# Hybrid decoder layer: values and output features first for one token tile, the last tile's mean from the weights' row sums

## The chip, the cores and the metric

The kernel runs on one core of one Trainium2 chip. The metric is the device time of one execution in microseconds; several runs are given by their median. A profiled execution gives, beside its own time, the span from the first to the last instruction and what each engine did in it: PE (TensorE, matmuls, with its weight loads as PEld), DVE (VectorE), ACT (ScalarE), POOL (GpSimd) and SP, whose queue issues most DMAs.

## The reference

One layer of a hybrid decoder trunk, all in float32, with 512 prompt tokens and 8 sample tokens (one new token for each of 8 running sequences):

```python
h = jnp.einsum('bte,ed->btd', x, w_in)          # 1024 -> 3600 columns
qa, ka, va, za, ga, qb, kb, vb, gb = jnp.split(h, split_points, axis=-1)
o_a = gla_chunked(qa, ka, va, log_a, s0, chunk) # gated linear attention, 4 heads, then RMS norm
o_b = dilated_attention(...)                    # 8 heads of 64, three (window, dilation) patterns
mix = concat([o_a * silu(ga), o_b * silu(gb)])
y = jnp.einsum('bte,ed->btd', mix, w_out)       # 1024 -> 1024
x_new = layer_norm(ALPHA * x + y, ln_g, ln_b)   # over the 1024 features
```

Outputs are the new residual stream of prompt and sample tokens, the states of the linear attention, and the window keys and values. The change touches three places: the two value projections `va` and `vb` (512 columns each), the output projection, and the layer norm of the last 128 prompt tokens.

## The kernel before

**Precision.** Each float32 operand of a large matmul is split into a high part (rounded to the type fp32r) and a low part (the rest). A product is three matmuls, high by high, high by low and low by high, accumulated over the eight 128-row tiles k of the contraction (`three`, line 622). So a unit of output, one PSUM bank, is 24 matmuls. A matmul has a stationary operand of up to 128 columns, which a weight load brings into the array, and a moving operand that streams past it.

**Tokens.** The 520 tokens stand in the columns of `xh` and `xl` in the order: prompt tiles 0 and 1 (256 columns), the 8 sample tokens, prompt tiles 2 and 3. The first 264 columns are one half, `TS[0]`, with `TW[0]` = 264; the last 256 are the other.

**Feature first or token first.** Where the weights are stationary and the tokens stream, the result has features in its partitions; the sample tokens ride along as eight more columns. Where a tile of 128 tokens is stationary and the weights stream, the result has tokens in its partitions. Values and output are wanted token first, but the sample tokens are wanted feature first. `token` (line 640) therefore does the first half of the tokens feature first: for each of two feature blocks of 128 a unit of 24 matmuls with 264 moving columns. `turn` (line 659) copies the 256 prompt columns out of PSUM and turns them with two PE transposes for each block. Tiles 2 and 3 are then done token first, 24 matmuls with 256 moving columns each. There are four such groups: `vb0`, `vb1`, `va0`, `va1`. The evacuations are made by `vb_into` (line 1102), which also splits the values and stores them, and `va_into` (line 1085).

**Output projection.** Mix tiles, split like all operands, meet the weights `wo[0]` and `wo[1]`, 512 columns each. `out_first` (line 1512) does eight units feature first, 128 features and 264 tokens each; the first five take their k tiles 0 to 3 (attention) one after another, then their k tiles 4 to 7 (linear attention), so that the latter may come later. `out_turn` (line 1533) copies a unit, keeps the eight sample columns in `yts` and turns the rest by two transposes. `out_unit` (line 1500) does tiles 2 and 3 token first: (2, 0) and (2, 512) and (3, 0) with 512 moving columns, (3, 512) and (3, 768) with 256.

**Layer norm.** `out_evac` (line 1552) adds a piece from PSUM to ALPHA times the residual and takes statistics for every 256 columns. When a tile's four are there, `norm` (line 1599) merges them, takes the reciprocal root by Ln and Exp on ACT and one Newton step, centres, scales and stores. For the last tile the Newton step runs on ACT, and the final pass is cut in three, each with its own store.

**What sets the order.** The kernel's tasks are generators. A planner in Python (`Plan`, line 197) runs them at build time: it asks each task for its next instruction, estimates when that could start by a cost for each kind of instruction (`Op`, line 82) and fixed delays between engines (lines 76 to 80), and issues the one that could start first; ties go by the priorities `PRIO` (line 72), where a lower number comes first. All queues are therefore written in the order the planner chose. `At(name, n)` holds a task in planning until a mark was set n times; it is no wait on the chip, where only the data dependencies count. `dense` (line 695) is the one task that writes nearly all large matmuls in a fixed sequence: queries, keys, values `vb`, gates `gb`, values `va`, gates `ga`, output. `split` (line 416) and `Group` (line 459) load weights and split them, the high part on ACT, the low part on DVE. `keys_store`, `ln_rows` and `residual` (lines 1065, 1480, 1489) issue the key stores, the loads of the norm's rows, and the loads of the residual tiles.

Every instruction is issued at line 368, so a profile's rows are told apart by tile names: `ps_vb_f` and `ps_va_f` are the feature-first units of the values, `ps_vb` and `ps_va` the token-first ones, `ps_yf` and `ps_y` the same for the output, `ps_turn` and `ps_yt` their transposes.

Of the kernel before, what the change touches and what calls it, by code (L numbers as in the profile page):

```python
# [72 lines left out]
    wload=3, wsplit=4, decay=48.3, res_s=8, res=8, level=22, keys_out=2, logit=25.7, value=20, fills=9, bias_table=7.3, gla_levels=7.6, gla_diagonal=7.7, gla_state=24, gla_queries=25, strips=14, sample_queries=48, sample_softmax=8.7, sample_values=46, sample_gla=11, mix_sample_a=8.7, mix_sample_b=16, ln_rows=17, keys_store=17.5, gla_out=26, sample_v=9.2, mix_tiles=33.5, scores=31, softmax=34.2, weighted=30, mix_a=18, mix_b=19, norm3=11, norm=9)  # L73


FROM_POOL = 1000.0
TO_PE, FROM_PE, OTHER, AFTER_DMA, WITHIN = 600.0, 250.0, 150.0, 500.0, 120.0
LATE = 600.0
# [294 lines left out]
def trunk(ctx: ExitStack, tc: tile.TileContext, xT, xp, xs, state, ck, cv, w_in, wab, gnorm,  # L373
# [61 lines left out]
    eps, minus3 = cst("eps", [P, 1]), cst("minus3", [P, 1])  # L435
# [23 lines left out]
    class Group:  # L459
# [20 lines left out]
        def part(self, name):  # L480
            tags = ("w",)
            if self.src is w_out:

                tags += ("sv",) * (plan.marks["sample"] == 2) + ("pt",) * (plan.marks["ob1"] == HB) + ("g",)
            return (yield Need(tags, name + self.name, [P, self.kk, self.w], F32R, spare=tags[-1] == "g"))

        def split(self, i, raw):
            a = yield from self.part(f"hi{i}_")
            b = yield from self.part(f"lo{i}_")
            self.tiles.append((a, b))  # L490
            n = self.n
            for k in range(0, self.kk, n):
                yield from split(raw[:, k:k + n, :], a[:, k:k + n, :], b[:, k:k + n, :])
# [111 lines left out]
    def fills():  # L605
        yield V.memset(rb.bitcast(F32)[64:66], 1.0)
        yield V.memset(eps, LN_EPS)
        yield V.memset(minus3, -3.0)
# [31 lines left out]
    def token(g, evac_f, evac):  # L640

        for f in range(2):
            fs = slice(f * P, f * P + P)
            ps = yield bank("d", f"ps_{g.name}f{f}")
            for k in range(KT):
                yield g.at(k)
                h, l = xh[k][:, TS[0]], xl[k][:, TS[0]]
                yield from three(ps[:, :TW[0]], k, ((g.hi[k][:, fs], h), (g.hi[k][:, fs], l), (g.lo[k][:, fs], h)))
            add(evac_f(ps, f), 2)
        for t in (2, 3):  # L650
            ps = yield bank("d", f"ps_{g.name}{t}")
            ts = slice(NB + t * P, NB + t * P + P)
# [6 lines left out]
    def turn(ps):  # L659

        f = yield Need("t1", "feat", [P, GW])
        yield copy(f, ps[:, :GW])
        free(ps)
        o = yield bank("t", "ps_turn")
        for t in range(2):
            yield T.transpose(o[:, t * P:t * P + P], f[:, t * P:t * P + P], ident)
        return o, f
# [27 lines left out]
    def dense():  # L695
# [47 lines left out]
        units = [(g, f) for g in range(4) for f in range(2)]  # L743
# [321 lines left out]
    def keys_store():  # L1065

        yield At("kw", 8)
        yield At("y0_done", 1)
# [16 lines left out]
    def va_into(i):  # L1085
        def evac_f(ps, f):
            c = slice(i * GW + f * P, i * GW + f * P + P)
            yield copy(vat[:, 2 * i + f, :], ps[:, GW:TW[0]])
            mark("vat")
            ps, f_t = yield from turn(ps)  # L1090
            free(f_t)
            yield copy(B["va0"][:, :, c], ps[:, :GW].rearrange("p (t c) -> p t c", t=2))
            mark("va_done")
            free(ps)

        def evac(ps, t):
            yield copy(B["va1"][:, t - 2, i * GW:i * GW + GW], ps)
            free(ps)
            mark("va_done")
        return evac_f, evac  # L1100

    def vb_into(i):
        def parts_of(o, x):
# [3 lines left out]
        def evac_f(ps, f):  # L1107
            c = slice(i * GW + f * P, i * GW + f * P + P)
            yield copy(vnt[:, 2 * i + f, :], ps[:, GW:TW[0]])
            mark("vnt")  # L1110
            ps, raw = yield from turn(ps)
            yield from parts_of(B[f"vhl{i}0"][:, :, 2 * f:2 * f + 2], ps[:, :GW].rearrange("p (t h d) -> p t h d", t=2, d=64))
            mark(f"vb{i}0")
            yield copy(raw, ps[:, :GW])
            free(ps)
            yield D.dma_start(vw_p[:GW, c].rearrange("(t p) c -> p t c", p=P), raw.rearrange("p (t c) -> p t c", t=2))
            free(raw)

        def evac(ps, t):
            yield from parts_of(B[f"vhl{i}1"][:, t - 2], ps.rearrange("p (h d) -> p h d", d=64))  # L1120
            mark(f"vb{i}1")
# [5 lines left out]
        return evac_f, evac  # L1127
# [352 lines left out]
    def ln_rows():  # L1480
        yield At("y0_done", 1)
# [7 lines left out]
    def residual(t):  # L1489
# [7 lines left out]
        yield D.dma_start(y, xp[t * P:t * P + P, :])  # L1497
        mark(f"y{t}")

    def out_unit(t, c, w):  # L1500
        u, tl, cs = t // 2, slice((t % 2) * P, (t % 2) * P + P), slice(c % 512, c % 512 + w)
        g = wo[c // 512]
        ps = yield bank("d", f"ps_y{t}{c // GW}")
        for k in range(KT):
# [4 lines left out]
            yield from three(ps[:, :w], k, ((mh, hi), (mh, lo), (ml, hi)))  # L1509
        add(out_evac(t, c // GW, ps[:, :w]), 2)  # L1510

    def out_first(*units):
# [3 lines left out]
        for g, f in units:  # L1516
            ps.append((yield bank(("d", "s"), f"ps_yf{g}{f}")))
            yield from out_half(g, f, ps[-1], range(4))
        for (g, f), p in zip(units, ps):
            yield from out_half(g, f, p, range(4, KT))  # L1520
            add(out_turn(g, f, p), 2)

    def out_half(g, f, ps, ks):
        w, c = wo[g // 2], g % 2 * GW + f * P
        for k in ks:
# [3 lines left out]
            mh, ml = (B[f"m{x}{'ba'[k // 4]}0"][:, k % 4, :] for x in "hl")  # L1529
# [3 lines left out]
    def out_turn(g, f, ps):  # L1533
        feat = yield Need("t1", "feat_y", [P, GW])
        yield copy(feat, ps[:, :GW])
        yield copy(yts[:, 2 * g + f, :], ps[:, GW:TW[0]])
        mark("yts")
        free(ps)
        if f == 0:
            yield from make(f"yt{g}", bank("t", f"ps_yt{g}"))  # L1540
        else:
            yield At(f"yt{g}")
        for t in range(2):
            yield T.transpose(B[f"yt{g}"][:, t * GW + f * P:t * GW + f * P + P], feat[:, t * P:t * P + P], ident)
        free(feat)
        mark(f"yt_in{g}")
        if plan.marks[f"yt_in{g}"] == 2:
            plan.share(B[f"yt{g}"], 2)
            for t in range(2):
                add(out_evac(t, g, B[f"yt{g}"][:, t * GW:t * GW + GW]), 2)  # L1550

    def out_evac(t, g, ps):
# [8 lines left out]
        if plan.marks[f"y{t}_done"] == 4:  # L1561
            add(norm(t), PRIO["norm3"] if t == 3 else PRIO["norm"])
# [36 lines left out]
    def norm(t):  # L1599
# [4 lines left out]
        var, last = mv[:, 1:2], t == 3  # L1604
# [5 lines left out]

        def centre(c):
            yield V.scalar_tensor_tensor(y[:, c], y[:, c], mv[:, 0:1], B["gamma"][:, c], op0=ALU.subtract, op1=ALU.mult)

        def finish(c):
            return V.scalar_tensor_tensor(y[:, c], y[:, c], rstd, B["beta"][:, c], op0=ALU.mult, op1=ALU.add)

        yield At("ln", 3)
        if last:
            cs = [slice(0, 512), slice(512, 768), slice(768, DM)]
            yield S.activation(nt[:, 0:1], rstd, AF.Square)  # L1620
            yield S.activation(nt[:, 0:1], nt[:, 0:1], AF.Identity, scale=x, bias=minus3)
            yield S.activation(rstd, nt[:, 0:1], AF.Identity, scale=rstd)
            mark("last")
            yield from centre(cs[0])
            yield from centre(slice(512, DM))
        else:
            cs = [slice(0, DM)]
            yield from centre(cs[0])
            yield V.scalar_tensor_tensor(nt[:, 0:1], rstd, x, rstd, op0=ALU.mult, op1=ALU.mult)
            yield V.scalar_tensor_tensor(rstd, nt[:, 0:1], -3.0, rstd, op0=ALU.add, op1=ALU.mult)  # L1630
        free(nt)
        for i, c in enumerate(cs):
            yield finish(c)
            yield (S if last and i == 1 else D).dma_start(y_p[t * P:t * P + P, c], y[:, c])
# [27 lines left out]
    add(ln_rows(), PRIO["ln_rows"])  # L1662
    add(keys_store(), PRIO["keys_store"])
# [108 lines left out]
```

## Time and profile before

| what | value |
|---|---|
| median of 3 runs | 288.28 us (288.16 to 288.7) |
| profiled execution, its own time | 287.84 us |
| its span, first to last instruction | 286.1 us |
| mean granted TensorE clock | 0.997 |
| PE busy | 274.8 us (96%), 2638 matmuls |
| weight loads | 259.1 us (91%), 2638 |
| DVE, ACT, POOL busy | 223.5, 172.1, 59.6 us |
| HBM traffic | 179 GB/s over the span |

A matmul's busy time in the profile is the time from its start to its modelled end, about 0.28 us for 256 columns, though the next one starts 0.12 us later. So PE's busy time hides short gaps, and the distance between starts is the better measure of what a matmul costs.

### The profile page before, as it was taken

What the parts mean: (1) busy time and instruction counts of PE and PEld (TensorE: products, weight loads), DVE (VectorE), ACT (ScalarE), POOL (GpSimd) and SP (SyncE); (2) the same over time, 40 slices, a digit from 0 to 9 for tenths busy, and PEclk for the clock granted to TensorE, in tenths of its full rate; (3) what the DMA queues carried; (4) which work ended last, traced back from release to release, by engine and by line L of the source; (5) the groups of instructions that cost most, each with busy time, mean ns of one, the idle gap of its engine ahead of it and who ended that gap; (6) DMA issues with size and microseconds to landing.
All of it is one profiled execution on the core that took longest, in us unless ns stands there. A gap on an engine that the chain in (4) does not pass through costs nothing.

```text
span 286.1 us, 6902 instructions
## 1 busy us (share of the span) xinstructions
PE 274.8 (96%) x2638; PEld 259.1 (91%) x2638; DVE 223.5 (78%) x546; ACT 172.1 (60%) x481; POOL 59.6 (21%) x74
## 2 busy tenths in 40 slices
PE   8999999999999999999999999899999999999991
PEld 5999999999989899998999999799899999997890
DVE  4923887899999989989889897765698895439845
ACT  5726565456877887696888685435689774212002
POOL 4000000002945907200047635540000000000000
PEclk9999999999999999999999999999999999999998
DMA  6963643337738687527996858768193796751112
GB/s 205 341 167 93 203 111 105 91 110 221 244 88 297 194 256 240 159 83 214 264 235 200 261 157 231 198 169 229 52 255 115 208 313 236 124 170 73 78 76 92
DMA packets 58371, 51.20 MB, mean 179 GB/s; under 512 B 12750, under 2 KB 49752, under 8 KB 58338
## 3 DMA queue, kind: packets, MB, share of 16 engines
q1 hardware_dynamic: 57778, 50.36, 59.7%
q8 instruction: 21, 0.34, 0.5%
q10 hardware_dynamic: 560, 0.39, 0.4%
q14 instruction: 12, 0.10, 0.1%
HBM read 45.19 MB, written 6.05 MB: 179 GB/s over the span
## 4 chain that ended last, share of the span: by engine, by line
PE 67%; DVE 17%; ACT 9%; DMA 3%; issue 1%; SPq 1%; DVEq 0%; ACTq 0%
PE ps_qb L368 8%; PE ps_y L368 8%; PE ps_yf L368 7%; PE ps_gb L368 6%; PE ps_first L368 5%; PE ps_vb_f L368 4%; PE ps_vb L368 4%; PE ps_va L368 3%; PE ps_pv L368 3%; PE ps_pt L368 3%; PE ps_kb L368 2%; PE ps_qa L368 2%; ACT sg L368 2%; PE ps_s L368 2%; DMA raw_wo__3550<-in_w_out_dram 2%
## 5 line engine op out<-in xcount | busy, mean ns | idle before, releaser
L368 POOL TENSOR_TENSOR past<-past,qbc 128x256 f32<-128x256 f32 x32 | 29.0, 941 | 78.5 <-DMA past<-in_ck_dram 78.5
L368 POOL TENSOR_TENSOR vv<-vv,pb 128x256 f32<-128x256 f32 x32 | 26.3, 853 | 47.5 <-DVE gb_s L368 30.6
L368 ACT ACTIVATE pr<-pr,ms 128x128 f32<-128x128 f32 (+3 forms) x59 | 30.8, 548 | 4.5 <-DVE ms L368 4.4
L368 PE MATMUL ps_first<-xx,hi_first 128*128 128x264 f32 (+1 forms) x96 | 18.2, 289 | 0.4 <-DVE xx L368 0.3
L368 PEld LDWEIGHTS ps_first<-xx,hi_first 128*128 128x128 f32 x96 | 15.0, 190 | 1.4 <-DVE xx L368 0.5
L368 PE MATMUL ps_pt<-cf,pr 128*128 128x128 f32 x80 | 13.8, 280 | 1.2 <-DVE va L368 0.6
L368 DVE CUSTOM_DVE_ANT_0 pr<-ps_s,strip 128x128 f32<-128x128 f32 (+3 forms) x32 | 14.3, 479 | 0.0
L368 PE MATMUL ps_first<-xx,lo_first 128*128 128x264 f32 (+1 forms) x48 | 13.5, 282 | 0.0
L368 ACT ACTIVATE sg<-sg 128x264 f32<-128x264 f32 (+1 forms) x32 | 13.4, 418 | 0.2
L368 ACT ACTIVATE rstd<-mv,eps 128x1 f32<-128x1 f32 x4 | 1.1, 291 | 18.6 <-DVE mv L368 18.6
L368 PEld LDWEIGHTS ps_pt<-cf,pr 128*128 128x128 f32 x80 | 9.1, 140 | 2.4 <-ACT pr L368 1.2
L368 DVE TENSOR_TENSOR ptl<-ps_pt,pth 128x384 fp32r<-128x384 f32 (+1 forms) x16 | 9.7, 618 | 1.9 <-ACT pth L368 1.8
L368 ACT ACTIVATE d<-d 128x512 f32<-128x512 f32 x13 | 7.7, 636 | 5.1 <-DVE d L368 5.1
L368 DVE TENSOR_REDUCE o_pv<-vv 128x4 f32<-128x1024 f32 x8 | 9.7, 1212 | 0.6 <-POOL vv L368 0.6
L368 DVE TENSOR_REDUCE lt<-past 128x16 f32<-128x1024 f32 x8 | 9.6, 1210 | 0.0
L368 DVE TENSOR_TENSOR d<-b 128x1024 f32<-128x1024 f32 x7 | 9.0, 1290 | 0.0
L368 DVE TENSOR_TENSOR obT<-ps_pv,pvl 64x256 f32<-64x256 f32 x16 | 6.6, 415 | 3.0 <-ACT pvl L368 2.9
L368 PEld LDWEIGHTS ps_first<-xx,lo_first 128*128 128x128 f32 x48 | 9.0, 188 | 0.0
L368 ACT COPY feat_y<-ps_yf 128x256 f32<-128x256 f32 x7 | 2.6, 373 | 10.6 <-PE ps_yf L368 10.6
L368 PE MATMUL ps_s<-kp,qh 64*128 64x128 f32 (+3 forms) x64 | 8.5, 345 | 0.0
L368 ACT CAST pth<-ps_pt 128x384 fp32r<-128x384 f32 (+1 forms) x16 | 8.2, 532 | 0.1
L368 PE MATMUL ps_pv<-pth,vhl 128*128 128x256 f32 (+1 forms) x32 | 7.7, 272 | 0.0
(542 smaller groups left out, 1067.8 us busy)
## 6 DMA issues: line engine op xcount, KB each, us to landing
past<-in_ck_dram SPq DMA_DIRECT2D x8, 512.0 KB
vv<-in_cv_dram SPq DMA_DIRECT2D x8, 512.0 KB, 4.9
pb<-psd_s SPq DMA_DIRECT2D x16, 256.0 KB, 4.2
qbc<-qsd SPq DMA_DIRECT2D x8, 256.0 KB, 5.5
strip<-tabr SPq DMA_DIRECT2D x8, 256.0 KB, 3.1
y<-in_xp_dram SPq DMA_DIRECT2D x4, 512.0 KB
x_raw<-in_xT_dram SPq DMA_DIRECT2D x7, 260.0 KB
out_dram<-y SPq DMA_DIRECT2D x3, 512.0 KB, 2.6
```

The lines of the kernel that those rows point to most:

```text
L368: getattr(eng.eng, op.fn)(*op.args, **op.kw)
```

## The change

1. **Values, feature first for one token tile.** `token` takes only tile 1 with the 8 sample tokens feature first (136 moving columns instead of 264). Tile 0 joins tiles 2 and 3 as a token-first unit. `turn` has one transpose for each feature block, and both blocks share one bank.
2. **Output, the same.** `out_first` gets eight units of 136 moving columns for tile 1 and the sample tokens, and `out_unit` does tile 0 token first in two units of 512 columns. The first group of five is (0, 0) and four feature units.
3. **Last token tile.** Its pieces are now 512, 256, 128 and 128 columns, the 256-wide one (3, 768) before (3, 512) and (3, 640). The sum of a tile's output over its features is a product of the mix with the row sums of `w_out`. `row_sums` forms those of `wo[1]` on ACT, in 16 passes of 512 columns with accumulation, splits them, and writes them into two more columns of the weight tiles. The piece (3, 768) streams 258 columns, and one of its extra columns yields the sum of the second 512 output columns for each token. The residual's part and the first 512 columns' part are summed on ACT.
4. **Its layer norm.** With the mean known before the last two pieces, `last_evac` takes each piece's squares around the mean on ACT as it comes, centres it on DVE, and after the last piece forms the variance, Ln, Exp and a Newton step on DVE.
5. **Order.** `keys_store` and `ln_rows` wait for three marks of `y0_done` instead of one. Most priorities and two constants of the planner have other values.

```diff
 PRIO = dict(
-    wload=3, wsplit=4, decay=48.3, ..., ln_rows=17, keys_store=17.5, gla_out=26, sample_v=9.2, mix_tiles=33.5, scores=31, softmax=34.2, weighted=30, mix_a=18, mix_b=19, norm3=11, norm=9)
+    wload=12.1, wsplit=5.9, decay=31.1, ..., ln_rows=8.4, keys_store=17.1, gla_out=17.7, sample_v=26.4, mix_tiles=27.7, scores=39.6, softmax=27.8, weighted=50.7, mix_a=38.6, mix_b=57.6, norm3=8.7, norm=15.3)
-FROM_POOL = 1000.0
+FROM_POOL = 300.0
-LATE = 600.0
+LATE = 900.0
...
-    def token(g, evac_f, evac):
+    def token(g, own, evac):
...
-                h, l = xh[k][:, TS[0]], xl[k][:, TS[0]]
-                yield from three(ps[:, :TW[0]], k, ((g.hi[k][:, fs], h), (g.hi[k][:, fs], l), (g.lo[k][:, fs], h)))
-            add(evac_f(ps, f), 2)
-        for t in (2, 3):
+                h, l = xh[k][:, P:TW[0]], xl[k][:, P:TW[0]]
+                yield from three(ps[:, :P + NB], k, ((g.hi[k][:, fs], h), (g.hi[k][:, fs], l), (g.lo[k][:, fs], h)))
+            add(turn(g.name, ps, f, own[:, f, :], evac), 2)
+        for t in (0, 2, 3):
...
-        yield from out_first(*units[:5])
-        for x in units[5:]:
+        yield from out_first((0, 0), 0, 1, 2, 3)
+        for x in ((0, 512), 4, 5, 6, 7):
             yield from out_first(x)
-        for t, c, w in ((2, 0, 512), (2, 512, 512), (3, 0, 512), (3, 512, GW), (3, 768, GW)):
+        for t, c, w in ((2, 0, 512), (2, 512, 512), (3, 0, 512), (3, 768, GW), (3, 512, P), (3, 640, P)):
             yield from out_unit(t, c, w)
...
-            yield from three(ps[:, :TW[0]], k, ((hi, mh), (lo, mh), (hi, ml)))
+            yield from three(ps[:, :P + NB], k, ((hi, mh), (lo, mh), (hi, ml)))
...
+    def row_sums():
+        yield At("y0_done", 1)
+        w_sums, w_sum = cst("w_sums", [P, 2, KT]), cst("w_sum", [P, KT])
+        junk = yield Need("g", "junk", [P, 2, 512])
+        for k in range(KT):
+            yield wo[1].at(k)
+            for j, l in enumerate((wo[1].hi, wo[1].lo)):
+                yield S.activation(junk[:, j], l[k][:, :512].bitcast(F32), AF.Identity, accum_out=w_sums[:, j, k:k + 1])
...
+            yield S.copy(a[:, :, 512:], x)
+            yield V.tensor_tensor(b[:, :, 512:], x, a[:, :, 512:].bitcast(F32), op=ALU.subtract)
+        mark("row_sums")
+
+    def last_evac(c, w, ps):
...
+        if c == 768:
+            yield At("mean_0")
+            yield V.scalar_tensor_tensor(mean3[:, 0:1], ps[:, w:w + 1], 1.0 / DM, mean3[:, 2:3], op0=ALU.mult, op1=ALU.add)
...
+        yield V.scalar_tensor_tensor(y[:, cs], y[:, cs], ALPHA, ps[:, :w], op0=ALU.mult, op1=ALU.add)
...
+        yield S.activation(B["squares"][:, cs], y[:, cs], AF.Square, scale=1.0 / 32, bias=bias3, accum_out=sq3[:, n:n + 1])
+        mark("squares")
+        yield V.scalar_tensor_tensor(B["centred"][:, cs], y[:, cs], mean3[:, 0:1], B["gamma"][:, cs], op0=ALU.subtract, op1=ALU.mult)
...
+        yield S.activation(r, sq3[:, 3:4], AF.Ln, bias=var3[:, 1:2])
+        yield S.activation(r, r, AF.Exp, scale=-0.5)
+        mark("last")
+        yield V.tensor_scalar(x, sq3[:, 3:4], var3[:, 1:2], None, op0=ALU.add)
+        yield V.scalar_tensor_tensor(x, r, x, r, op0=ALU.mult, op1=ALU.mult)
+        yield V.scalar_tensor_tensor(r, x, -3.0, r, op0=ALU.add, op1=ALU.mult)
+        for i, c in enumerate((slice(0, 512), slice(512, 768), slice(768, DM))):
+            yield V.scalar_tensor_tensor(z[:, c], z[:, c], r, B["beta"][:, c], op0=ALU.mult, op1=ALU.add)
+            yield (S if i == 1 else D).dma_start(y_p[3 * P:, c], z[:, c])
```

More of the change, by code (lines that the diff above doesn't have):

```diff
@@ L72 @@
 PRIO = dict(
-    wload=3, wsplit=4, decay=48.3, res_s=8, res=8, level=22, keys_out=2, logit=25.7, value=20, fills=9, bias_table=7.3, gla_levels=7.6, gla_diagonal=7.7, gla_state=24, gla_queries=25, strips=14, sample_queries=48, sample_softmax=8.7, sample_values=46, sample_gla=11, mix_sample_a=8.7, mix_sample_b=16, ln_rows=17, keys_store=17.5, gla_out=26, sample_v=9.2, mix_tiles=33.5, scores=31, softmax=34.2, weighted=30, mix_a=18, mix_b=19, norm3=11, norm=9)
-FROM_POOL = 1000.0
+    wload=12.1, wsplit=5.9, decay=31.1, res_s=18.3, res=28.2, level=22.5, keys_out=2, logit=35.7, value=28.9, fills=59.4, bias_table=37.7, gla_levels=11.8, gla_diagonal=17.1, gla_state=27, gla_queries=21.6, strips=26.7, sample_queries=8.4, sample_softmax=8.4, sample_values=38.6, sample_gla=7.7, mix_sample_a=4.9, mix_sample_b=14.8, ln_rows=8.4, keys_store=17.1, gla_out=17.7, sample_v=26.4, mix_tiles=27.7, scores=39.6, softmax=27.8, weighted=50.7, mix_a=38.6, mix_b=57.6, norm3=8.7, norm=15.3)
+FROM_POOL = 300.0
 TO_PE, FROM_PE, OTHER, AFTER_DMA, WITHIN = 600.0, 250.0, 150.0, 500.0, 120.0
-LATE = 600.0
+LATE = 900.0
 SWITCH = 230.0
@@ L492, in split @@
             for k in range(0, self.kk, n):
-                yield from split(raw[:, k:k + n, :], a[:, k:k + n, :], b[:, k:k + n, :])
+                yield from split(raw[:, k:k + n, :], a[:, k:k + n, :self.w], b[:, k:k + n, :self.w])
                 self.hi += [a[:, j, :] for j in range(k, k + n)]
@@ L657, in token, with turn @@
         g.done(1)
-    def turn(ps):
-        f = yield Need("t1", "feat", [P, GW])
-        yield copy(f, ps[:, :GW])
-        free(ps)
[L664 to L667, printed above, removed]
+    def turn(n, ps, f, own, evac):
+        feat = yield Need("t1", "feat", [P, P])
+        yield copy(feat, ps[:, :P])
+        yield copy(own, ps[:, P:P + NB])
+        mark("vnt" if n[1] == "b" else "vat")
+        free(ps)
+        if f == 0:
+            yield from make("turn_" + n, bank("t", "ps_turn"))
+        else:
+            yield At("turn_" + n)
+        o = B["turn_" + n]
+        yield T.transpose(o[:, f * P:f * P + P], feat, ident)
+        free(feat)
+        if f:
+            add(evac(o[:, :GW], 1), 2)
     def sample_rows(x, rows):
@@ L1085, in va_into, with evac @@
     def va_into(i):
[L1086 to L1094, printed above, removed]
         def evac(ps, t):
-            yield copy(B["va1"][:, t - 2, i * GW:i * GW + GW], ps)
+            yield copy(B[f"va{t // 2}"][:, t % 2, i * GW:i * GW + GW], ps)
             free(ps)
             mark("va_done")
-        return evac_f, evac
+        return vat[:, 2 * i:2 * i + 2, :], evac
     def vb_into(i):
-        def parts_of(o, x):
+        def evac(ps, t):
+            o, x = B[f"vhl{i}{t // 2}"][:, t % 2], ps.rearrange("p (h d) -> p h d", d=64)
             yield S.copy(o[..., 0, :], x)
             yield V.tensor_tensor(o[..., 1, :], x, o[..., 0, :].bitcast(F32), op=ALU.subtract)
[L1107 to L1121, printed above, removed]
+            mark(f"vb{i}{t // 2}")
             raw = yield Need("t1", "vb_raw", [P, GW])
@@ L1497, in residual, with out_unit @@
         yield D.dma_start(y, xp[t * P:t * P + P, :])
+        if t == 3:
+            junk = yield Need("t2", "junk_y", [P, 512])
+            yield S.activation(junk, y[:, 512:], AF.Identity, scale=ALPHA / DM, accum_out=mean3[:, 1:2])
+            free(junk)
         mark(f"y{t}")
-    def out_unit(t, c, w):
-        u, tl, cs = t // 2, slice((t % 2) * P, (t % 2) * P + P), slice(c % 512, c % 512 + w)
+    def out_unit(t, c, w, ps=None, ks=range(KT)):
+        first = (t, c) == (3, 768)
+        if first:
+            yield At("row_sums")
+        n = w + 2 * first
+        u, tl, cs = t // 2, slice((t % 2) * P, (t % 2) * P + P), slice(c % 512, c % 512 + n)
         g = wo[c // 512]
-        ps = yield bank("d", f"ps_y{t}{c // GW}")
-        for k in range(KT):
+        ps = ps or (yield bank("d", f"ps_y{t}{c // P}"))
+        for k in ks:
             yield g.at(k)
@@ L1508, in out_unit, with out_half @@
             hi, lo = g.hi[k][:, cs], g.lo[k][:, cs]
-            yield from three(ps[:, :w], k, ((mh, hi), (mh, lo), (ml, hi)))
-        add(out_evac(t, c // GW, ps[:, :w]), 2)
+            yield from three(ps[:, :n], k, ((mh, hi), (mh, lo), (ml, hi)))
+        if KT - 1 in ks:
+            add(last_evac(c, w, ps) if t == 3 else out_evac(t, c // GW, ps[:, :w]), 2)
     def out_first(*units):
         ps = []
[L1516 to L1524, printed above, removed]
+        for ks in range(4), range(4, KT):
+            for i, x in enumerate(units):
+                if ks[0] == 0:
+                    ps.append((yield bank(("d", "s"), f"ps_yf{i}")))
+                if isinstance(x, tuple):
+                    yield from out_unit(*x, 512, ps[i], ks)
+                else:
+                    yield from out_half(x, ps[i], ks)
+    def out_half(m, ps, ks):
+        w, c = wo[m // 4], m % 4 * P
         for k in ks:
@@ L1528, in out_half @@
             yield At(f"mix_s{'ba'[k // 4]}")
-            mh, ml = (B[f"m{x}{'ba'[k // 4]}0"][:, k % 4, :] for x in "hl")
+            mh, ml = (B[f"m{x}{'ba'[k // 4]}0"][:, k % 4, P:] for x in "hl")
             hi, lo = w.hi[k][:, c:c + P], w.lo[k][:, c:c + P]
-            yield from three(ps[:, :TW[0]], k, ((hi, mh), (lo, mh), (hi, ml)))
[L1533 to L1536, printed above, removed]
+            yield from three(ps[:, :P + NB], k, ((hi, mh), (lo, mh), (hi, ml)))
@@ L1537, in out_turn @@
+        if KT - 1 in ks:
+            add(out_turn(m, ps), 2)
+    def out_turn(m, ps):
+        feat = yield Need("t1", "feat_y", [P, P])
+        yield copy(feat, ps[:, :P])
+        yield copy(yts[:, m, :], ps[:, P:P + NB])
         mark("yts")
         free(ps)
-        if f == 0:
-            yield from make(f"yt{g}", bank("t", f"ps_yt{g}"))
-        else:
-            yield At(f"yt{g}")
-        for t in range(2):
-            yield T.transpose(B[f"yt{g}"][:, t * GW + f * P:t * GW + f * P + P], feat[:, t * P:t * P + P], ident)
+        n = f"yt{m // 2}"
+        if m % 2 == 0:
+            yield from make(n, bank("t", "ps_" + n))
+        else:
+            yield At(n)
+        yield T.transpose(B[n][:, m % 2 * P:m % 2 * P + P], feat, ident)
@@ L1545, in out_turn @@
         free(feat)
[L1546 to L1550, printed above, removed]
+        mark(n + "_in")
+        if plan.marks[n + "_in"] == 2:
+            add(out_evac(1, m // 2, B[n][:, :GW]), 2)
+    def row_sums():
[6 more added lines that the diff above has]
+                yield S.activation(junk[:, j], l[k][:, :512].bitcast(F32), AF.Identity, accum_out=w_sums[:, j, k:k + 1])
+        free(junk)
+        yield V.tensor_tensor(w_sum, w_sums[:, 0], w_sums[:, 1], op=ALU.add)
+        for i, (a, b) in enumerate(wo[1].tiles):
+            x = w_sum[:, 2 * i:2 * i + 2, None].to_broadcast([P, 2, 2])
+            yield S.copy(a[:, :, 512:], x)
+            yield V.tensor_tensor(b[:, :, 512:], x, a[:, :, 512:].bitcast(F32), op=ALU.subtract)
+        mark("row_sums")
@@ new lines, in last_evac @@
+    def last_evac(c, w, ps):
+        yield At("y3")
+        y, cs = B["y", 3], slice(c, c + w)
+        n = plan.marks["last_evac"]
+        mark("last_evac")
+        if n == 0:
+            B["centred"] = yield Need("g", "centred", [P, DM])
+            B["squares"] = yield Need("g", "squares", [P, DM])
+        if c == 768:
+            yield At("mean_0")
+            yield V.scalar_tensor_tensor(mean3[:, 0:1], ps[:, w:w + 1], 1.0 / DM, mean3[:, 2:3], op0=ALU.mult, op1=ALU.add)
+            yield V.tensor_scalar(bias3, mean3[:, 0:1], -1.0 / 32, None, op0=ALU.mult)
+            mark("mean")
+        yield V.scalar_tensor_tensor(y[:, cs], y[:, cs], ALPHA, ps[:, :w], op0=ALU.mult, op1=ALU.add)
+        free(ps)
+        if c == 0:
+            junk = yield Need("t2", "junk_0", [P, 512])
+            yield S.activation(junk, y[:, cs], AF.Identity, scale=1.0 / DM, accum_out=mean3[:, 0:1])
+            free(junk)
+            yield V.tensor_tensor(mean3[:, 2:3], mean3[:, 0:1], mean3[:, 1:2], op=ALU.add)
+            mark("mean_0")
+        yield At("mean")
+        yield At("ln", 3)
+        yield S.activation(B["squares"][:, cs], y[:, cs], AF.Square, scale=1.0 / 32, bias=bias3, accum_out=sq3[:, n:n + 1])
+        mark("squares")
+        yield V.scalar_tensor_tensor(B["centred"][:, cs], y[:, cs], mean3[:, 0:1], B["gamma"][:, cs], op0=ALU.subtract, op1=ALU.mult)
+        if n == 2:
+            yield At("squares", 3)
+            yield V.tensor_reduce(var3[:, 1:2], sq3[:, :3], axis=AX.X, op=ALU.add)
+            yield V.tensor_scalar(var3[:, 1:2], var3[:, 1:2], LN_EPS, None, op0=ALU.add)
+        if n < 3:
+            return
+        x, r, z = var3[:, 0:1], var3[:, 2:3], B["centred"]
+        yield S.activation(r, sq3[:, 3:4], AF.Ln, bias=var3[:, 1:2])
[7 more added lines that the diff above has]
+            yield (S if i == 1 else D).dma_start(y_p[3 * P:, c], z[:, c])
+        free(y, z, B["squares"])
@@ L1603, in norm @@
         yield V.bn_aggr(mv, st.rearrange("p a b -> p (a b)"))
-        var, last = mv[:, 1:2], t == 3
+        var = mv[:, 1:2]
         nt = yield Need("m", "newton", [P, 2])
@@ L1609, in norm @@
         yield V.tensor_scalar(x, var, LN_EPS, None, op0=ALU.add)
[L1611 to L1615, printed above, removed]
         yield At("ln", 3)
[L1618 to L1630, printed above, removed]
+        yield V.scalar_tensor_tensor(y, y, mv[:, 0:1], B["gamma"], op0=ALU.subtract, op1=ALU.mult)
+        yield V.scalar_tensor_tensor(nt[:, 0:1], rstd, x, rstd, op0=ALU.mult, op1=ALU.mult)
+        yield V.scalar_tensor_tensor(rstd, nt[:, 0:1], -3.0, rstd, op0=ALU.add, op1=ALU.mult)
         free(nt)
-        for i, c in enumerate(cs):
-            yield finish(c)
-            yield (S if last and i == 1 else D).dma_start(y_p[t * P:t * P + P, c], y[:, c])
+        yield V.scalar_tensor_tensor(y, y, rstd, B["beta"], op0=ALU.mult, op1=ALU.add)
+        yield D.dma_start(y_p[t * P:t * P + P, :], y)
         free(y)
```

19 lines of the change are left out of this document (10 added, 9 removed).

## The prediction

> **What bounds the kernel now.** I read the page first, for the share of each engine and the chain that ended last.
>
> ```profile
> span 286.1 us, 6902 instructions
> PE 274.8 (96%) x2638; PEld 259.1 (91%) x2638; DVE 223.5 (78%) x546; ACT 172.1 (60%) x481; POOL 59.6 (21%) x74
> PE 67%; DVE 17%; ACT 9%; DMA 3%; issue 1%; SPq 1%; DVEq 0%; ACTq 0%
> ```
>
> PE works nearly without a break, and there are as many weight loads as matmuls: a stationary tile that serves two matmuls in a row is loaded twice. PE is the resource to count. Next come its waits, which are all that a better order could give back.
>
> ```profile
> PEld ps_va_f L368 <- DVE lo_va__2973 L368: 1.7, 2, 1.2
> PEld ps_pt L368 <- ACT pr L368: 1.2, 3, 0.8
> PEld ps_oa L368 <- DVE oa L368: 0.8, 1, 0.8
> PEld ps_yf L368 <- DVE ga L368: 0.5, 1, 0.5
> PE ps_pt L368 <- DVE va L368: 0.6, 1, 0.6
> ```
>
> Those from the value stage on (all but the second) make 3.6 us. So I price each matmul by the time from its start to the next one's. The chain in order of time (start, duration, what) and the timeline (start, duration of one) give it:
>
> ```profile
> 247.32 2.93 PE ps_yf L368 x24
> ...
> 190.81 4.51 PE ps_va L368 x38
> ...
> 34.37 0.44 PE ps_dg L368 x4
> ```
>
> ```profile
> 262.55 0.39 PE L368 MATMUL ps_y<-hi_wo__3619,mhb 128*128 128x512 f32 x1
> ...
> 264.41 0.39 PE L368 MATMUL ps_y<-hi_wo__3679,mlb 128*128 128x512 f32 x1
> ```
>
> 264 moving columns cost 2.93/24 = 0.122 us, 256 cost 4.51/38 = 0.1187, a PE transpose 0.44/4 = 0.11, and 512 columns (8 steps between the two rows) 1.86/8 = 0.2325. Between 256 and 512 that is proportional to the columns. The change brings 136 and 128 columns, and there the proportion need not hold. Two places show it. First, the values' weighting, where a 128-column pair precedes a 256-column one:
>
> ```profile
> 136.67 0.22 PE L368 MATMUL ps_pv<-pth,vhl 128*128 128x128 f32 x1
> 136.68 0.13 PEld L368 LDWEIGHTS ps_pv<-ptl,vhl 128*64 128x64 f32 x1
> 136.73 0.22 PE L368 MATMUL ps_pv<-ptl,vhl 128*64 128x128 f32 x1
> 136.73 0.19 PEld L368 LDWEIGHTS ps_pv<-pth,vhl 128*128 128x128 f32 x1
> 136.79 0.33 PE L368 MATMUL ps_pv<-pth,vhl 128*128 128x256 f32 x1
> 136.84 0.19 PEld L368 LDWEIGHTS ps_pv<-ptl,vhl 128*128 128x128 f32 x1
> ...
> 136.96 0.28 PE L368 MATMUL ps_pv<-ptl,vhl 128*128 128x256 f32 x1
> ```
>
> Streaming 128 columns takes 0.06 us (136.67, .73, .79). A load starts as soon as the matmul ahead of it has started, never earlier. The load of 128 weight columns that begins at 136.73 holds its matmul: issued at 136.79 that one lasts 0.33 instead of 0.28, the next load starts only at 136.84, and the next matmul comes 0.17 later instead of 0.12. So a 128-column load needs 136.84 - 136.73 = 0.11 us, hidden behind 256 columns but not behind 128. A 64-column load (0.13 against 0.19) is short enough. Second, the scores of the first query tile stream 128 columns three times in a row, two row halves side by side; these are the loads:
>
> ```profile
> 81.98 0.19 PEld L368 LDWEIGHTS ps_s<-kp,qh 64*128 64x128 f32 x2
> 82.09 0.19 PEld L368 LDWEIGHTS ps_s<-kp,ql 64*128 64x128 f32 x2
> 82.21 0.19 PEld L368 LDWEIGHTS ps_s<-kp,qh 64*128 64x128 f32 x2
> ```
>
> One step is 0.11 to 0.12. **A matmul of 128 or 136 columns with a fresh 128-column load costs 0.112 us**, hardly less than one of 256.
>
> Last, the tail, from the chain of waits:
>
> ```profile
> 278.81 0.43 DVE y L368
> ...
> 280.03 0.30 ACT rstd L368
> 280.33 0.02 issue
> 280.35 0.21 ACT rstd L368
> ...
> 281.57 0.75 DVE y L368
> ```
>
> From the last evacuation (278.81) to the first finishing pass (281.57) are 2.76 us.
>
> **The change part by part.** The sum is made against the profiled execution, 287.84 us (span 286.1 and 1.74 around it); the median of the runs, 288.28, lies 0.44 above. The moving columns stay the same in total; what changes is how they are cut.
>
> *Values (`token`, four groups).* Feature-first matmuls shrink from 264 to 136 columns, a third token-first unit of 24 matmuls is added, two transposes go: 48 x 0.112 + 24 x 0.1187 - 48 x 0.122 - 2 x 0.11 = 5.38 + 2.85 - 5.86 - 0.22 = +2.15 us a group, +8.6 in all.
>
> *Output features (`out_first`).* 192 matmuls go from 264 to 136 columns, two units of 512 columns (48 matmuls) are added, eight transposes go: 192 x 0.112 + 48 x 0.2325 - 192 x 0.122 - 8 x 0.11 = 21.5 + 11.16 - 23.42 - 0.88 = +8.4 us.
>
> *Last token tile.* Two pieces of 256 become one of 258 and two of 128: 24 x 0.12 + 48 x 0.112 - 48 x 0.1187 = +2.55 us. These are bound by the load too, since the stationary mix tile has 128 columns.
>
> PE therefore gets 8.6 + 8.4 + 2.55 = +19.5 us. All of it lies on the chain, because PE has little idle time in these stages. Bounds: with 0.108 a short matmul 1.7 less over 432 of them, with 0.116 1.7 more.
>
> *Tail.* The statistics, their merge and three ScalarE steps leave it. What remains is one 128-column evacuation, a Square with accumulation, Ln, Exp, two tiny DVE steps. Their nearest rows:
>
> ```profile
> 202.13 0.35 DVE L368 SCALAR_TENSOR_TENSOR oa<-va,dg,ps_oa 128x128 f32<-128x128 f32 x1 [2.67 <-PE ps_oa L368]
> ...
> 202.51 0.31 ACT L368 ACTIVATE sq<-oa 128x128 f32<-128x128 f32 x1 [2.29 <-DVE oa L368]
> ...
> 202.73 0.19 ACT L368 ACTIVATION_READ_ACCUMULATOR sq<-oa 128x1 f32 x1
> ```
>
> ```profile
> 270.70 0.21 DVE L368 SCALAR_TENSOR_TENSOR newton<-rstd,newton 128x1 f32<-128x1 f32 x1
> ...
> 271.14 1.28 DVE L368 SCALAR_TENSOR_TENSOR y<-y,rstd,beta 128x1024 f32<-128x1024 f32 x1
> ```
>
> 0.35 + 0.41 (202.51 to the end of the read at 202.92) + 0.30 + 0.21 + 0.44 (270.70 to 271.14) and four gaps of 0.02 = 1.79, so **-0.97 us**. The centring and the first two pieces' squares lie under the last piece's 2.7 us of matmuls. The finishing passes and stores are as before.
>
> *Row sums.* Sixteen ScalarE passes over 512 columns with an accumulator read, and a wait of the last tile's first piece for them. Behind that wait on PE stand only the last pieces. The nearest 512-wide pass lasts
>
> ```profile
> L368 ACT ACTIVATE d<-d x13: 615/624/684, 43.7 to 77.7; 128x512 f32<-128x512 f32 x13
> ...
> 240.00:260.00 20.00, 20.00 (x151) 18.89 (x150) 10.29 (x31) 5.87 (x18) 0.00 (x0) 1.00 0.58 152
> ```
>
> so 16 x (0.62 + 0.19) = 13 us at most, in a stage where ACT (fourth busy column) idles 14 of 20 us, and PE's growth adds more. I take 0; without that cover the piece waits up to 13 us. The sums' write into the weight tiles waits for matmuls that read them and may hold PE for moments: 0 to +2.
>
> *Moved DMAs.* Gamma, beta and the 16 key stores now follow the third mark of y0, and the loads of y2 and y3 queue behind them on SP:
>
> ```profile
> 237.56 13.00 SPq L368 DMA_DIRECT2D out_dram<-kw  x16
> 250.66 0.92 SPq L368 DMA_DIRECT2D y<-in_xp_dram  x2
> ```
>
> Between that mark and the first use of y2 lie four short units (4 x 24 x 0.112 = 10.8 us) and one of 512 (5.6). The 13.9 us of issues leave 2.5 us for landing, so y2's evacuation may come late, but the next 5.6 us unit has its own bank: 0.
>
> *Fewer small copies on ACT and DVE; new priorities and planner constants.* These rewrite the order on every queue. It cannot be counted from rows. It gains at most the waits above; it loses where a weight or a softmax comes late, about as much as the worst DMA wait in the chain:
>
> ```profile
> 224.21 4.61 DMA raw_wo__3550<-in_w_out_dram
> ```
>
> Bounds -3.6 to +4.6. A longer PE stage also gives the weight splits more time, so I take -2.0.
>
> Sum: 19.5 - 0.97 - 2.0 = +16.6 us; 287.84 becomes 304.4, and on the scale of the median 288.28 + 16.6 = **304.9 us**.
>
> **The rivals.**
>
> *Loads hidden (the other side).* If loads reached two matmuls ahead, a short matmul would cost its stream, 0.06 (0.064 for 136 columns). Values: 48 x 0.064 + 2.85 - 5.86 - 0.22 = -0.16, four times -0.6; output: 12.3 + 11.16 - 23.42 - 0.88 = -0.85; last tile +0.05. With the tail -2.4 us: 285.9, faster. For it: the two 0.06 steps of the weighting. Against it: the 0.17 that follows them, and the scores' loads. It decides once a run of 128-column loads goes below about 0.07.
>
> *Loads partly hidden.* If in long runs the queue smooths the loads, the step lies between 0.06 and 0.112, say 0.086: 432 x 0.026 = 11.2 us less, 293.7. For it only that the rows here are short runs; against it that no load starts before the preceding matmul. The Trainium skill ("TensorE: Matmul & The Clock Gate", section "Back-to-back issue gap") speaks for this one: it gives about 81 ns for a sustained matmul of 128 columns, load included; by it the sum would be 13.4 us lower, an estimate of 291.5. The scores' steps of 0.11 to 0.12 do not agree with it. Its section "LDWEIGHTS" has the load take the columns over 1.2, 107 ns for 128, which is the 0.11 of the rows.
>
> *The new order starves PE.* A late weight or a late mix tile costs more than PE's growth covers; two waits of 4.6 us on top: above 310. For it: loads and splits of weights lose urgency (`wload` 3 to 12.1, `wsplit` 4 to 5.9). Against it: PE takes longer per weight in the value and output stages.
>
> **How the numbers follow.** Forecast 0.82, loads hidden 0.08, partly hidden 0.04, starved 0.06. What a measurement of this kernel tells from no change is about 0.2%. Faster 0.08, same 0.01 (a mixture of the first two), slower 0.91. The range takes the forecast with its bounds (-1.7, -1.6 and an order that gains more than I took; +1.7, +2, +2 of order): 298 to 310.
>
> **What would show it.** Right: short matmuls of `ps_vb`, `ps_va` and `ps_yf` start 0.11 us apart, PE's span to the last product grows by about 17 us, the tail shrinks by 1. Wrong: starts 0.06 to 0.09 apart (a rival on loads), or PE gaps of microseconds behind DVE, ACT or DMA (the order). If PE grows as said and the span doesn't, the chain was not PE's.

## The result

The changed kernel takes **301.6 us** (median of five, 301.45 to 301.93) beside 288.28 for the kernel before: ratio 1.0464, 95% interval 1.0442 to 1.0485. It is slower by 13.3 us. The forecast was 304.9 with a range of 298 to 310, so the sign, the price of the short matmuls and the range held; 3.3 us of the size did not.

The page of the changed kernel, its span, PE and the shares of the chain that ended last:

```profile
span 299.7 us, 7270 instructions
PE 291.1 (97%) x2790; PEld 275.4 (92%) x2790; DVE 224.6 (75%) x567; ACT 180.1 (60%) x512; POOL 55.3 (18%) x74
PE 87%; DVE 6%; ACT 3%; DMA 1%; SPq 1%; issue 1%; DVEq 0%
```

There are 152 more matmuls (168 more products, 16 fewer transposes), as the diff says, and the chain has become PE's nearly throughout: 87% instead of 67%. The work of DVE and ACT hardly grew.

The chain in order of time (start, duration, what) shows what a matmul costs now. The first and third rows are units of 136 moving columns, the second is of 256, the last is the end of tile 2 and all of tile 3:

```profile
186.40 4.31 PE ps_va_f L368 x39
...
193.00 7.50 PE ps_va L368 x64
...
260.80 2.64 PE ps_yf L368 x24
...
273.62 19.56 PE ps_y L368 x120
```

136 columns cost 4.31/39 = 0.1105 and 2.64/24 = 0.11 us a matmul, 256 columns 7.50/64 = 0.117. So 136 columns instead of 256 save 6%. The last row is the same by the prices of the prediction: 48 x 0.2325 + 24 x 0.12 + 48 x 0.112 = 19.4.

The timeline shows why, each weight load beside its matmul:

```profile
260.75 0.19 PEld L368 LDWEIGHTS ps_yf<-mha,hi_wo__3973 128*128 128x128 f32 x1
260.81 0.28 PE L368 MATMUL ps_yf<-mha,hi_wo__3973 128*128 128x136 f32 x1
260.86 0.19 PEld L368 LDWEIGHTS ps_yf<-mha,lo_wo__3974 128*128 128x128 f32 x1
260.92 0.27 PE L368 MATMUL ps_yf<-mha,lo_wo__3974 128*128 128x136 f32 x1
260.97 0.19 PEld L368 LDWEIGHTS ps_yf<-mla,hi_wo__3973 128*128 128x128 f32 x1
261.03 0.28 PE L368 MATMUL ps_yf<-mla,hi_wo__3973 128*128 128x136 f32 x1
```

Loads follow each other every 0.11 us. A matmul's row starts 0.06 us after its load began, when the one ahead has streamed its columns, but the next load starts only 0.05 us later: the matmul has to wait that long for its weights. A stream (0.06 us) and the load for the next matmul (0.11 us) begin together and run side by side, so each step lasts as long as the longer of the two, the load. If they ran one after the other, a step would take 0.17 us.

The tail, from the chain of waits:

```profile
293.20 0.30 DVE y L368
...
293.53 0.50 ACT squares L368 x2
...
294.06 0.30 ACT var L368
...
295.07 0.75 DVE centred L368
```

From the last evacuation to the first finishing pass are 1.87 us, 0.89 less than before.

One view is empty now. The kernel before had 2.7 us of waits named on PE itself after 95 us (total, times, longest):

```profile
PE ps_va_f L368 <- DVE lo_va__2973 L368: 1.2, 2, 1.0
PE ps_pt L368 <- DVE va L368: 0.6, 1, 0.6
PE ps_oa L368 <- DVE oa L368: 0.6, 1, 0.6
PE ps_yf L368 <- DVE ga L368: 0.3, 1, 0.3
```

The changed kernel has none between 95 us and its last product. To see what that is worth I added up, for each group of tiles, the distances from a matmul's start to the next one's, and set beside them the bare price (counts times the prediction's prices: 0.112, 0.1187, 0.122, 0.2325, 0.11 for a transpose):

| PE, us | before | bare | after | bare |
|---|---|---|---|---|
| values (`ps_vb`, `ps_va`, their `_f`, turns) | 52.5 | 48.0 | 57.1 | 56.6 |
| gates `ps_gb` | 24.4 | 23.1 | 24.3 | 23.1 |
| softmax and weighting (`ps_s`, `ps_pt`, `ps_pv`) | 27.3 | | 26.8 | |
| output features (`ps_yf`, `ps_yt`) | 25.9 | 25.2 | 33.4 | 33.5 |
| output by token (`ps_y`) | 22.8 | 22.4 | 25.5 | 25.0 |

The changed kernel's distances come out at the bare price within 0.5 us in each of the three changed rows, so the prices hold. But the kernel before lay 4.5 us above it in the value stage and 0.7 in the output features, and the changed one lies 0.5 above it and nothing there. So the start of the last product moved by 14.4 us (278.50 to 292.89), not by the 19.5 of the counted work. Of these 5 us the forecast had taken 2.0.

Not all of the 4.5 us were lost in the value stage. Three pauses make 2.4 of them (steps of 0.90, 0.51 and 1.30 us at 171.44, 182.91 and 184.13), and 2.4 more lie in 28 steps of 0.20 to 0.23 us. Of these, 21 follow a transpose whose own step is only about 0.03 us: the next matmul's row starts so soon, but its load isn't done, and the time is booked one row later. (For the one that starts at 123.17 the load begins at 123.14, the next load 0.11 us later at 123.25, and the next matmul starts at 123.37.) Such a pair together costs what the two prices add up to, 0.03 + 0.20 = 0.11 + 0.12. Since 14 of these transposes belong to other rows, the softmax above all, 1.2 of the 4.5 us belong there, and some 3.3 us were lost in the value stage. The loss also differs from trace to trace: the same values took 50.9 to 52.0 us in the traces of the output features alone and of the last tile alone (both below).

### The profile page after: what moved, and what is told of

Read it like the earlier page. It is cut to its first block, busy times and chain, and to the rows that moved or that the text cites. A ratio compares the mean times of both kernels' runs of the same rounds, so it can differ in the third digit from the quotient of the medians.

```text
span 299.7 us, 7270 instructions
## 1 busy us (share of the span) xinstructions
PE 291.1 (97%) x2790; PEld 275.4 (92%) x2790; DVE 224.6 (75%) x567; ACT 180.1 (60%) x512; POOL 55.3 (18%) x74
## 4 chain that ended last, share of the span: by engine, by line
PE 87%; DVE 6%; ACT 3%; DMA 1%; SPq 1%; issue 1%; DVEq 0%
PE ps_yf L368 11%; PE ps_y L368 8%; PE ps_ga L368 8%; PE ps_gb L368 8%; PE ps_qb L368 8%; PE ps_vb L368 6%; PE ps_va L368 6%; PE ps_first L368 5%; PE ps_va_f L368 4%; PE ps_pv L368 3%; PE ps_vb_f L368 3%; PE ps_kb L368 3%; PE ps_pt L368 3%; PE ps_s L368 2%; PE ps_qa L368 2%; PE ps_oa L368 2%
## 5 line engine op out<-in xcount | busy, mean ns | idle before, releaser
L368 POOL TENSOR_TENSOR vv<-vv,pb 128x256 f32<-128x256 f32 x32 | 27.0, 876 | 57.0 <-DMA pb<-psd_s 52.3
L368 ACT ACTIVATE pr<-pr,ms 128x256 f32<-128x256 f32 (+3 forms) x52 | 27.5, 550 | 5.3 <-DVE ms L368 5.1
L368 POOL TENSOR_TENSOR past<-past,qbc 128x256 f32<-128x256 f32 x32 | 24.0, 786 | 33.7 <-DMA past<-in_ck_dram 33.7
L368 POOL MEMSET att<- 64x512 f32 x2 | 1.0, 522 | 57.4 <-DVE ks L368 57.4
L368 ACT COPY pvl<-ps_pv 64x256 f32<-64x256 f32 x16 | 5.6, 370 | 5.6 <-PE ps_pv L368 5.3
L368 DVE TENSOR_TENSOR pt<-ps_pt,pt 128x128 fp32r<-128x128 f32 (+1 forms) x16 | 5.4, 352 | 3.0 <-ACT pt L368 2.9
```

Source lines behind the costliest of these rows:

```text
L368: getattr(eng.eng, op.fn)(*op.args, **op.kw)
```

## The experiments

Theory: PE sets the time, and a matmul costs the longer of its stream and its load of 128 columns, 0.11 us. The rivals: the stream alone counts (0.064 us); or every matmul has a fixed cost of about 0.11 us whatever it loads. For the missing 5 us: they vanish under PE's longer stages (cover), or the new priorities remove them (order).

**Loads of half the width.** Each feature unit of the output is cut in two halves of 64 stationary columns; the result is the same, with twice the matmuls.

```diff
-            hi, lo = w.hi[k][:, c:c + P], w.lo[k][:, c:c + P]
-            yield from three(ps[:, :P + NB], k, ((hi, mh), (lo, mh), (hi, ml)))
+            for r in (0, 64):
+                hi, lo = w.hi[k][:, c + r:c + r + 64], w.lo[k][:, c + r:c + r + 64]
+                o = ps[:64, 4 * r:4 * r + P + NB]
+                for i, (x, z) in enumerate(((hi, mh), (lo, mh), (hi, ml))):
+                    yield T.matmul(o, x, z, start=k == 0 and i == 0, stop=k == KT - 1 and i == 2, ...)
```

> The changed kernel with each feature unit of the output projection cut in two halves of 64 stationary columns, 384 matmuls of 136 moving columns in place of 192. Theory 'load': a load of 64 columns hides behind the stream, a matmul costs 0.064 us, 24.6 instead of 21.5 us, 304.7 us in all. Rival 'fixed cost': a matmul costs about 0.11 us whatever is loaded, +21.5 us, 323 us.

Measured: 305.4 us (two runs). The chain of this kernel, one feature unit of 48 matmuls:

```profile
265.97 3.06 PE ps_yf L368 x48
```

3.06/48 = 0.064 us. The moving operand is unchanged, 136 columns; the load was halved, and the matmul went from 0.11 to 0.064. So it is the load, not a fixed cost, and the stream price for 136 columns is the one that the rival had. The halves also write 64 rows of the result instead of 128; that this isn't the cause is seen in the prediction's rows, where the matmul at 136.67, with all 128 stationary columns, is followed after 0.06 us by one with a load of 64. The halves still lose, since there are twice as many.

**The change's parts one at a time**, each on the kernel before with its order constants.

Values alone (`token`, `turn` and the two evacuations from the changed kernel):

```diff
-                yield from three(ps[:, :TW[0]], k, ...)
+                yield from three(ps[:, :P + NB], k, ...)
...
-        for t in (2, 3):
+        for t in (0, 2, 3):
```

> The kernel before, with the change's value groups alone (tile 1 and the sample tokens feature first, tiles 0, 2, 3 token first) and the order constants of before. By the load theory PE's work grows by 4 x 2.15 = 8.6 us; the waits for the values' weight splits (some 2 to 3 us in the profile before) may go under it. 294 to 297 us. Rival 'stream': no growth, 288 us.

Measured: 297.9 us (ratio 1.0373, 1.0329 to 1.0417), +9.8 us. The growth of the work is there. The waits of the value stage went (57.2 us of distances against a bare 56.6), but others came: 26.1 us in the gates `ps_gb` instead of 24.4, 27.8 in the output features instead of 25.9. So the old order gave nothing back on the whole, and the expectation's top was passed by 0.9.

Output features alone, with the key stores and the norm's rows behind the third mark of `y0_done` as in the change:

```diff
-        units = [(g, f) for g in range(4) for f in range(2)]
-        yield from out_first(*units[:5])
-        for x in units[5:]:
+        yield from out_first((0, 0), 0, 1, 2, 3)
+        for x in ((0, 512), 4, 5, 6, 7):
```

> The kernel before, with the change's output features alone (eight units of 136 columns, tile 0 in two units of 512 columns), the last tile's norm and the order constants as before. By the load theory PE's work grows by 8.4 us, with at most 1 us of waits to give back: 295.5 to 296.5 us. Rival 'stream': 287.5 us.

Measured: 295.9 us (1.0272, 1.0244 to 1.0299), +7.9 us, as the load theory has it.

The last tile alone, with pieces of 258, 128 and 128 columns:

```diff
-        ... (3, 0, 512), (3, 512, GW), (3, 768, GW)):
+        ... (3, 0, 512), (3, 768, GW), (3, 512, P), (3, 640, P)):
```

> The kernel before, with the change's last token tile alone, its last pieces 258, 128 and 128 columns, and the order constants of before. PE's work +2.55 us (48 matmuls of 128 columns bound by their loads), tail -0.9: 289.7 us. Rival 'stream': 287.2 us, as with two pieces of 256 columns.

Measured: 289.4 us (1.0057, 1.0038 to 1.0076), +1.3 us: 2.6 for the narrow pieces less the shorter tail. The three parts make 9.8 + 7.9 + 1.3 = 19.0 us.

**The last tile with wide pieces.** The same, but the last two pieces keep 258 and 256 columns, so that only the tail changes.

```diff
-        ... (3, 768, GW), (3, 512, P), (3, 640, P)):
+        ... (3, 768, GW), (3, 512, GW)):
...
-        if n == 2:
-            yield At("squares", 3)
+        if n == 1:
+            yield At("squares", 2)
```

> The kernel before, values and output features as before, with only the last tile's mean by a column of row sums and its squares on ScalarE; its last two pieces stay 256 columns wide (258 and 256). PE's work grows by 0.03 us. Theory 'tail is apart': the tail shortens by 0.7 to 1.0 us and 287.4 us result. Rival 'row sums cost': the 16 accumulating passes and the writes into the weight tiles hold PE or displace evacuations, 288.5 us or more.

> The same kernel as in the run with pieces of 258 and 256 columns, timed again beside the others, because its interval still held no change: 0.6 to 0.8 us faster than before, if the shorter tail is all it does.

Measured: 287.44 us (0.9979, 0.9954 to 1.0004) and 287.30 us (0.9984, 0.9963 to 1.0004). Its chain of waits:

```profile
278.80 0.43 DVE y L368
...
280.90 0.75 DVE centred L368
```

2.10 us from the last evacuation to the first finishing pass instead of 2.76, so 0.66 less where 0.7 to 1.0 had been expected. Both medians lie 0.6 to 0.8 us under the kernel before, which fits that, but each interval just holds 1. Taken together, the 24 executions have a mean 0.55 us below that of the 39 executions of the kernel before (95% interval about 0.2 to 0.9). So it is the one version that seems to beat both kernels, by a fifth of a per cent; the second series was added because the first left the question open, so this is weaker than one series planned for it.

**The order, both ways.** First the changed kernel with the priorities and constants of before:

```diff
-    wload=12.1, wsplit=5.9, decay=31.1, ...
+    wload=3, wsplit=4, decay=48.3, ...
-FROM_POOL = 300.0
+FROM_POOL = 1000.0
-LATE = 900.0
+LATE = 600.0
```

> The changed kernel with the priorities and planner constants of before. PE's work is that of the changed kernel (+19.5 us). Theory 'cover': the waits of the value and output stages vanish because PE takes longer there, whatever the order; 301.6 us within 1.5, and PE's waits for weight splits stay under 1 us. Theory 'order': the new priorities gave back what the prediction had not counted; 304 to 306 us, with the waits of before back.

Measured: 305.8 us (1.0606, 1.0569 to 1.0644), 17.8 us over the kernel before. So the new order is worth 4.2 us on this structure. Yet the waits of the value stage are nearly gone here too (57.3 us of distances, bare 56.6). The constants are the old ones, so the new structure took these away, as the first theory said. Whether by PE's longer stages alone or also by the queues that the planner writes around them, no run separates. The loss sits elsewhere: 25.6 us in the gates, 28.3 in softmax and weighting, 34.7 in the output features, against 24.3, 26.8 and 33.4 in the changed kernel, 4.1 us together. Neither theory is right alone.

Then the kernel before with the new order:

> The kernel before with the priorities and planner constants of the changed one, nothing else. Theory 'cover': no gain without PE's longer stages, 288.3 us within 1.5. Theory 'order': the new order alone takes about 3 us of waits out, 285 us.

Measured: 292.2 us (1.0136, 1.0093 to 1.0179), **slower** by 4.1 us; both theories miss it. Its waits on PE after 95 us are new ones:

```profile
PE ps_pt L368 <- DVE obT L368: 0.9, 1, 0.9
PE ps_gb L368 <- DVE ms L368: 0.7, 2, 0.4
PE ps_ort L368 <- DVE o_r L368: 0.7, 1, 0.7
PE ps_yt L368 <- ACT feat_y L368: 0.6, 1, 0.6
PE ps_pt L368 <- DVE pt L368: 0.6, 2, 0.4
```

The same numbers gain 4.2 us on the one structure and lose 4.1 on the other. Here the order is worth something only on the structure that it came with.

**One priority.** Could one number give the kernel before what the whole order gave the changed one? Two tries on the version with wide pieces.

```diff
-    ... value=20, ...
+    ... value=40, ...
```

> The kernel before with the last tile's mean by a column and pieces of 258 and 256, and one priority changed: the sample values' long reductions on VectorE (value, 20 to 40) give way to other work. Theory 'one priority suffices': the weight splits of the values come earlier, PE's 1.2 us wait for them goes, 285.5 to 286.5 us. Rival 'orders are tuned as a whole': one changed number reshuffles queues far away and waits appear elsewhere, 288 us or more.

Measured: 288.9 us (1.0028, 1.0008 to 1.0048). The value stage got shorter (49.8 us of distances instead of 51.6), but a new wait came at the output weights:

```profile
PEld ps_yf L368 <- ACT hi_wo__3703 L368: 1.5, 1, 1.5
```

```diff
-    wload=3, wsplit=4, ...
+    wload=3, wsplit=2, ...
```

> The same kernel with the other single priority: the weight splits before all else but evacuations (wsplit, 4 to 2). Theory 'one priority suffices': the values' wait for splits goes, 286 us. Rival 'orders are tuned as a whole': 288 us or more.

Measured: 297.4 us (1.0317, 1.0292 to 1.0342), 10 us more than with the old number. PE lost in many places, most around the start of the output:

```profile
PE ps_yf L368 <- ACT mha L368: 1.7, 1, 1.7
PE ps_ort L368 <- DVE o_r L368: 1.2, 1, 1.2
PE ps_kb L368 <- DVE kw L368: 0.9, 1, 0.9
PE ps_og L368 <- DVE s L368: 0.8, 1, 0.8
```

"Orders are tuned as a whole" holds in both tries, two numbers of some 35. A part of both losses is a drop of PE's clock behind such waits (last section).

## Why the prediction was right, point by point

*The price of a short matmul* was the decisive step, and it was right: 0.112 us from a handful of rows of other tiles, 0.11 in the changed kernel's own. It was shown to be the load by halving the load (0.064).

*Values +8.6, output +8.4, last tile +2.55*: the bare columns of the table differ by as much, but they are made with the same prices. What supports the terms is that the changed kernel's distances (57.1, 33.4, 25.5) lie within 0.5 us of them. As kernels of their own the output came at +7.9 and the last tile with its tail at +1.3 (forecast 2.55 - 0.97 = 1.58); the values came at +9.8, since waits appeared behind them.

*Tail -0.97*: measured -0.89 in the chain. The evacuation from PSUM took 0.30 where the nearest row had said 0.35, and the Square with its read 0.50 instead of 0.41.

*Row sums at no cost*: right. Their passes on ACT run from 246.4 to 261.0 us, 0.62 to 0.64 us each with 0.19 to 0.20 for the read, and the piece that needs them starts at 284.8, 24 us after the last.

```profile
L368 ACT ACTIVATE junk<-hi_wo__3748 x2: 641/642/643, 246.4 to 248.9; 128x512 f32<-128x512 f32 x2
...
L368 ACT ACTIVATION_READ_ACCUMULATOR junk<-lo_wo__3974 x2: 193/193/193, 259.8 to 261.0; 128x1 f32 x2
```

*Moved DMAs at 0*: right. The last two residual loads leave SP at 257.49 us, land within 4.3 us, and the first use is at 274.4.

*Priorities and small copies, -2.0 with bounds -3.6 to +4.6*: this step was mis-sized. Work and tail together had been put at +18.5; the kernel came out at +13.3, so the step was worth -5.2. With the old order it was worth 17.8 - 18.5 = -0.7, and the new order gave the rest (4.2 us between the two medians; the 0.3 that are missing lie between the two series of runs). The bound failed because the prediction took the rows of named waits for all that an order could give back. It took 2.0 of their 3.6 us, but none of those rows is left, and more than they named is gone. (Of its second row, left out as lying ahead of the value stage, 0.8 us are at 172.31, the same pause as the fifth row.) On PE a wait is counted from the modelled end of the matmul ahead, 0.16 us behind the next one's earliest start (0.28 against 0.12), so a shorter pause shows neither as idle time nor as a wait. Distances between starts, which I used for the prices, would have shown in advance that the kernel before lay 4.5 us above the bare prices in the values and 0.7 in the output features, some 4 us of it real loss. The other bound was too small as well: on the version with wide pieces one priority cost 10 us.

*The range.* It held, but not by its terms alone. With this step at its bound of -3.6, and the work as it came out, the forecast would have been 303.3; the measured 301.6 lies below. The range reached to 298 because it also allowed for cheaper short matmuls, which didn't come, and, without a number, for an order that gains more.

*PE's span to the last product* was to grow by about 17 us and grew by 14.4, for the same reason; the short matmuls start 0.11 us apart, as said.

*The rivals.* Loads hidden and loads partly hidden fell with the 0.11 us steps. So did the sustained 81 ns for 128 columns of the Trainium skill ("TensorE: Matmul & The Clock Gate", section "Back-to-back issue gap") for these fp32r operands; the same page's section "LDWEIGHTS" agrees with them, and with the halved load. PE was not starved in the changed kernel, but the last two runs show that this rival was a real one.

## What to carry to other kernels

Price a matmul by the distance between starts, and compare its moving columns with its stationary ones: with float32-type operands here a fresh load of 128 columns takes 0.11 us, so anything under about 240 moving columns is paid by the load (an estimate: 0.11 us at the 0.2325/512 us a column of the widest matmuls). Cutting a 264-column unit in two saves next to nothing: each half costs 0.11 where the whole cost 0.122. Transposes that are saved (0.11 us each) weigh little against a unit of 24 such matmuls. Where short and long matmuls alternate, add the distances of neighbours up before calling one of them a loss. And a written order belongs to its structure: when the work of a stage changes, compare both structures each with its own order, and take no gain of a retuned order over to another kernel.

## What the runs showed of the hardware

A late operand can cost PE more than its wait. In the run with `value` at 40 PE waited twice, at 236.0 and 236.7 us, and from 237.62 on it ran at half its clock for 3.41 us. The busy time and granted clock by windows (start and end, length, PE busy, matmuls, clock, DMA share, GB/s):

```profile
234.21:237.62 3.41, 1.74 (x10) 1.00 0.31 118
...
237.62:241.03 3.41, 3.41 (x18) 0.50 0.70 181
241.10:245.00 3.90, 3.90 (x34) 1.00 1.05 307
```

In the 3.41 us ahead PE was busy for 1.74, half of the time; in the next 3.41 us it was fully busy but began only 16 matmuls (the 18 count those still running at its start) instead of 28. The timeline shows their distance, 0.22 us instead of 0.12:

```profile
237.72 0.42 PE L368 MATMUL ps_yf<-mha,hi_wo__3534 128*128 128x264 f32 x1
237.94 0.42 PE L368 MATMUL ps_yf<-mha,lo_wo__3535 128*128 128x264 f32 x1
```

So the waits of about 2 us cost another 1.7. Not every execution has this: three of the ten show a mean clock of 0.991 and took 289.0 to 290.4 us, the others 0.994 to 0.997 and 288.0 to 289.1. In the run with `wsplit` at 2 this happened twice:

```profile
163.55:166.96 3.41, 2.16 (x15) 1.00 1.00 293
166.97:170.37 3.40, 3.40 (x19) 0.50 1.07 254
```

```profile
245.50:252.20 6.70, 5.94 (x26) 0.50 0.99 278
```

Ahead of the second drop, from 242.08 to 245.50, PE was busy for 1.30 us. That makes 10.2 us at half clock in all, some 5 of the 12 us that this execution, the longest of the five at 299.4 us, lost against the old number. The mean clock of the other four, 0.982 to 0.991, shows that they lost as much or less this way. A busy time of 2.16 in such a stretch was followed by the drop here, while in the kernel before the 3.42 us from 182.0 on have 2.18 and no drop followed; what exactly decides was not tried. All twelve traces agree on one thing: by their clock records, a stretch at full clock lasts a whole number of 3.413 us, 13 to 87 of them. With windows laid out from these borders, each one in which PE was busy for 1.74 us or less was followed by half clock; of the five with 1.83 to 2.19 only the one named here was, and of the fuller ones none.

The Trainium skill ("TensorE: Matmul & The Clock Gate", section "What's actually happening") has the clock fall after an idle window of about 3.4 us; the length of 3.41 us agrees, but the windows ahead were not idle: PE was busy in 38 to 63% of them. The traces of the other kernels show no such drop before the last product.
